# A decoder block with product-key experts: dots of gathered rows over three blocks instead of two, a gate turn in two halves, a tile of its own for third parts, and last sums written behind the last low parts

## The chip, the cores and the metric

The kernel runs on one core of a Trainium2 chip. Its time is the device time of one execution in microseconds; several executions are summed up by their median. The engines are named as in the profile: PE (TensorE, with PEld for its weight loads), DVE (VectorE), ACT (ScalarE), POOL (GpSimd) and SP (SyncE, which here only issues transfers). Each of the engines runs its own list of instructions in order, and waits at an instruction until what it reads has been written and what it overwrites has been read.

## What is computed

One layer on 512 tokens of width 1024, in float32. Two mixers (windowed attention and gated linear attention) come first, and what the change touches comes behind them: a layer of 16384 experts, of which each token uses 128.

```python
q = (h @ wq).reshape(B, S, 8, 2, 128)
sub_scores = einsum('bshpk,hpnk->bshpn', q, subkeys)
top_v, top_i = lax.top_k(sub_scores, 16)                 # 16 of 128 keys, for two halves of the key
cand   = top_v[..., 0, :, None] + top_v[..., 1, None, :] # 16 x 16 candidates of each head
best_v, best_pos = lax.top_k(cand, 16)
expert = take_along_axis(top_i[0] * 128 + top_i[1], best_pos)
gates  = softmax(best_v)
...
ub  = take(u, expert)                                    # 128 rows of u for each token
hid = gelu(einsum('tkd,td->tk', ub, h)) * gates
out = einsum('tk,tkd->td', hid, take(v, expert))
x   = rms_norm(x + gate2 * out)
```

The number of an expert is a pair of keys, each 0 to 127.

## The kernel before

**Two ways through the expert layer.** The tokens stand in four blocks of 128. For the first three ("dense" blocks 0, 1, 2; `DENSE`, 384 tokens) the kernel doesn't gather rows: it multiplies with all 16384 rows of `u` (in parts of 128 experts, "u parts"), and later with all rows of `v`, with a matrix of gates that is zero where a token doesn't use an expert. For the fourth block (`GB`) it gathers the rows of `u` and `v` that are used. In between stand the last 64 tokens of block 2 (`SB` is block 2, `TS` = 64): their part on the side of `u` is gathered too, in 64 steps, each a gather of 128 rows (`sp_gather`, an indirect transfer that POOL issues into one of three buffers, tile `spr`) and a product of these rows with the tokens with a sum along the row (`sp_dot`, one DVE instruction, L1292 in the profile of before). `sp_dot(m)` issues the gather for step m + 3, into the buffer that it has just read. When all 64 are done, `sp_finish` takes the gelu on ACT, `sp_close` multiplies with the gates of these tokens on DVE and writes the result over the gates with two transfers on SP's queue (`g<-sphid`). On the side of `v` these 64 tokens are dense like the others.

**Stages.** Modulation, mixers and the product-key scores take until about 425 us. From there to 797 us runs the **gate stage**, to 1460 us the **v stage**, and then the end. In the gate stage run, woven into each other:

- the gate matrix of the dense blocks, by groups of eight tokens, 48 groups in all. A group has a one-hot of keys on DVE (`one_hot`, L1182, tile `o12`, for both keys of each token), a product of the second key's one-hot with two parts of the gates on DVE (L1200, tile `o2`; the gates are split into three bf16 parts), eight third parts on ACT (L1204, one for each token, the one-hot with a scale per row), 24 matmuls on PE (L1211, banks `pg`), and two evictions on ACT (L1213, tile `gs`). Four groups (32 tokens) make a write of 2 MB to memory (`Gd<-gs`).
- what prepares the gates of a block: `gate_transposes` turns the two key numbers and the gates on PE so that tokens lie along the free axis (tile `t12`, bank `trg`), `gate_parts` and `gate_rest` split the gates into the parts (`gp3` the two that the product uses, `gr3` the third).
- the u parts: a high part on ACT (L71, `his`) and a low part on DVE (L72, `los`) of a chunk of rows of `u`, 24 matmuls on PE (L78 to L80, bank `ph`), a gelu on ACT (L967), and a write of the results (`gsp<-ge`) on ACT's queue.
- the 64 gathers and dots.

**Who sets the order.** In this stage DVE's and POOL's instructions run in the order in which the program writes them: `work` is a chain of generators that yield the DVE and PE time of each piece by a table of costs (a dot 1.15, a product 1.2, ...), and between two pieces a loop writes u parts as long as PE's share of its planned work is behind DVE's (`p * DVE_ALL < (d + LEAD_U) * PE_ALL`). PE, ACT and SP are ordered by a scheduler on a timeline of its own. `woven(n, rows, extra, rest)` writes a block: for q = 0 to 7 (16 tokens each) `gate_group` yields four pieces (one-hot, product and what follows, twice), and after each piece one dot is written while there are `rows`; behind q come the pieces of `extra[q]`. Before, dots are written 13 times ahead of block 0 (`head`) and then four times per q in blocks 0 and 1, until the 64 are used up in block 1 at q = 4. There `sp_finish` and `sp_close` follow (`second_block`, q = 4 and 5), then the turn of block 2's gates (q = 6 and 7), and block 2 has no dots.

**The v stage and the end.** `prep(i)` makes step i of the v stage ready: it multiplies gates with gelus (`A`), makes high parts on ACT (`hi` L1642, `Ah` L1645) and low parts on DVE (`lo` L1651, `Al` L1658), writes dots of the gathered block in between (`gather_to`), and loads what comes next. `v_matmuls` then runs, for each of the step's two key numbers, three matmuls into each of six accumulators (L78 to L80, `acc`). Tiles for the low parts: `slots`, three in turn (`los` twice, `lo2`). Three of the steps have `extras`, pieces that belong to the fourth block: `gate2_rows` (a table for the output gate), `table` with `close_half` (sum, gate and residual of the gathered block, L1688 to L1689, and its squares on ACT), and `root`, `refine`, `finish` (the norm: L1695 to L1706 on DVE, Ln and Exp on ACT (L1698), and the output, L1721). They are written between a step's high and low parts. The last four v numbers (`LAST`) are multiplied block by block, so that the first blocks are closed while the others run; then `close_half` and the norm for the three dense blocks.

## Time and profile before

| what | value |
|---|---|
| three runs, median (lowest to highest) | 1487.56 us (1485.44 to 1487.62) |
| the profiled execution, its own time | 1493.26 us |
| span of its instructions | 1491.5 us |
| mean granted TensorE clock | 0.978 |
| PE busy | 1430.0 us, 96% of the span, 9019 matmuls |
| DVE busy | 1259.9 us, 84% |
| ACT busy | 715.3 us, 48% |
| POOL busy | 608.1 us, 41% |
| DMA | 443.82 MB, mean 298 GB/s |

The shares are means over stages that differ: PE, for one, is nearly full in the v stage and less so in the gate stage. So the profile is read by stages. A row of a group of instructions has: line, engine, operation, result <- operands with their tile names (numbers left out), shapes, count | busy time, mean ns of one | idle time of the engine just ahead of them, and what ended most of it. A row of the timeline has: start in us, length, engine, line, operation, and in brackets the idle time ahead and what ended it. A row of windows has: the stretch, its length, busy us (and instructions) of PE, PEld, DVE, ACT and POOL, then the granted clock, the share of the DMA engines, and GB/s.

### The profile page before, as it was taken

The page shows a single profiled execution, that of the slowest core. Times are in us where ns is not written, and L with a number is a line of the kernel's source. Part 1 is how long each engine was busy: PE and PEld are TensorE (multiplying, and loading weights), DVE is VectorE, ACT ScalarE, POOL GpSimd, SP SyncE. Part 2 cuts the span into 40 slices and gives each one's busy share as a digit, 9 for nine tenths or more (in the row PEclk, how much of TensorE's full clock was granted, in tenths as well). Part 3 has the DMA queues.
Part 4 walks back from the last instruction along what each step waited for, and adds up shares of the span by engine and source line. Part 5 has one row for each costly group of instructions (what it writes and reads, how often), then busy time and mean ns, then how long its engine had stood idle before and what let it go on. Part 6 is the DMA issues. An engine that isn't in the chain of part 4 may idle for free. (4 is left out here: it accounts for less than half of the span.)

```text
span 1491.5 us, 23906 instructions
## 1 busy us (share of the span) xinstructions
PE 1430.0 (96%) x9019; PEld 1269.2 (85%) x9019; DVE 1259.9 (84%) x2306; ACT 715.3 (48%) x1297; POOL 608.1 (41%) x401
## 2 busy tenths in 40 slices
PE   5999999999999998989988999999999999999996
PEld 4788787888899998989988888888888888888885
DVE  6777767589999788989765899989899998899985
ACT  4556376533344577757996333332333333323232
POOL 2000000044523444532003677667777676555430
PEclk9999899999999999999999999999999999999998
DMA  9522636344258899999669999999999999999952
GB/s 356 227 85 81 203 101 210 120 178 160 102 192 275 309 348 323 362 351 308 231 227 390 415 411 412 412 413 410 401 410 388 407 371 412 401 412 410 384 224 71
DMA packets 129971, 443.82 MB, mean 298 GB/s; under 512 B 11952, under 2 KB 48576, under 8 KB 109504
## 3 DMA queue, kind: packets, MB, share of 16 engines
q1 hardware_dynamic: 71120, 256.39, 45.8%
q0 software_dynamic: 47136, 171.99, 29.8%
q10 hardware_dynamic: 11600, 13.93, 2.6%
q8 instruction: 70, 1.15, 0.3%
q14 instruction: 45, 0.37, 0.1%
HBM read 399.70 MB, written 42.47 MB: 296 GB/s over the span
## 5 line engine op out<-in xcount | busy, mean ns | idle before, releaser
L78 PE MATMUL ph<-h2Th,his 128*128 128x320 f32 x1024 | 323.0, 316 | 7.8 <-ACT ge L967 5.2
L80 PE MATMUL ph<-h2Th,los 128*128 128x320 f32 x1024 | 320.0, 314 | 10.3 <-DVE los L72 8.5
L79 PE MATMUL ph<-h2Tl,his 128*128 128x320 f32 x1024 | 319.6, 312 | 0.0
L1338 POOL DMA_INDIRECT gu<-in_u_dram,ix_u x128 | 210.5, 1645 | 174.7 <-DVE gu L1348 79.0
L1373 POOL DMA_INDIRECT gv<-in_vP_dram,ix_v x128 | 211.6, 1653 | 119.9 <-DVE gacc L1378 89.0
L80 PEld LDWEIGHTS ph<-h2Th,los 128*128 128x128 f32 x1024 | 195.6, 191 | 12.3 <-DVE los L72 10.2
L78 PEld LDWEIGHTS ph<-h2Th,his 128*128 128x128 f32 x1024 | 196.1, 192 | 9.9 <-ACT ge L967 6.0
L79 PEld LDWEIGHTS ph<-h2Tl,his 128*128 128x128 f32 x1024 | 196.0, 191 | 0.8
L1286 POOL DMA_INDIRECT spr<-in_u_dram,spix x64 | 106.1, 1658 | 167.6 <-DVE spr L1292 122.6
L79 PE MATMUL acc<-los,Ah 128*128 128x512 f32 x432 | 169.2, 392 | 2.4 <-DVE los L1651 2.4
L80 PE MATMUL acc<-his,Al 128*128 128x512 f32 x432 | 169.2, 392 | 0.1
L78 PE MATMUL acc<-his,Ah 128*128 128x512 f32 x432 | 168.8, 391 | 0.0
L1378 DVE SCALAR_TENSOR_TENSOR gacc<-gv,hg,gacc 128x1024 f32<-128x1024 f32 x127 | 162.4, 1278 | 3.2 <-DMA gv<-in_vP_dram,ix_v 2.6
L1348 DVE SCALAR_TENSOR_TENSOR gu<-gu,h2n 128x1024 f32<-128x1024 f32 x128 | 155.3, 1217 | 3.9 <-DMA gu<-in_u_dram,ix_u 3.9
L78 PE MATMUL acc<-hi,Ah 128*128 128x512 f32 x336 | 131.6, 392 | 0.0
L80 PE MATMUL acc<-hi,Al 128*128 128x512 f32 x336 | 131.3, 391 | 0.0
L79 PE MATMUL acc<-lo,Ah 128*128 128x512 f32 x336 | 130.9, 390 | 0.0
L1204 ACT ACTIVATE o<-o,gr 128x128 bf16<-128x128 bf16 x384 | 126.0, 447 | 4.8 <-DVE o L1182 4.8
L1645 ACT ACTIVATE Ah<-gr 128x768 fp32r<-128x768 f32 x64 | 53.5, 836 | 141.5 <-PE acc L79 127.3
L71 ACT ACTIVATE his<-u 128x1024 fp32r<-128x1024 f32 x86 | 90.7, 1058 | 32.5 <-DMA u<-in_uT_dram 15.6
L72 DVE TENSOR_TENSOR los<-u,his 128x1024 fp32r<-128x1024 f32 x75 | 91.2, 1218 | 15.8 <-ACT his L71 15.8
L1292 DVE SCALAR_TENSOR_TENSOR spr<-spr,xs 128x1024 f32<-128x1024 f32 x64 | 77.9, 1220 | 26.7 <-DMA spr<-in_u_dram,spix 26.6
(617 smaller groups left out, 3013.7 us busy)
## 6 DMA issues: line engine op xcount, KB each, us to landing
u<-in_uT_dram SPq DMA_DIRECT2D x43, 1024.0 KB, 6.4
gr<-Gd SPq DMA_DIRECT2D x15, 1536.0 KB, 10.9
Gd<-gs SPq DMA_DIRECT2D x10, 2048.0 KB, 10.7
gsp<-ge ACTq DMA_DIRECT2D x40, 320.0 KB, 5.2
wa<-in_w_ada_dram SPq DMA_DIRECT2D x12, 1024.0 KB, 5.3
wo<-in_w_out_dram SPq DMA_DIRECT2D x8, 1024.0 KB, 6.0
wq<-in_wq_dram SPq DMA_DIRECT2D x8, 1024.0 KB, 7.2
wi<-in_w_in_dram SPq DMA_DIRECT2D x7, 1024.0 KB, 5.0
```

What stands on the lines that cost most here:

```text
L71: nc.scalar.activation(hi, src, AF.Copy)
L72: lo_eng.tensor_tensor(lo, src, hi, OP.subtract)
L78: nc.tensor.matmul(acc, lh, rh, start=start, stop=False)
L79: nc.tensor.matmul(acc, lh, rl, start=False, stop=False)
L80: return nc.tensor.matmul(acc, ll, rh, start=False, stop=stop)
L1204: nc.scalar.activation(o2[:, g, 2, :, r], o12[:, g, 1, :, r], AF.Copy, scale=low[:, 2 * g0 + i:2 * g0 + i + 1])
L1286: nc.gpsimd.indirect_dma_start(out=sp[m], out_offset=None, in_=a["u"], in_offset=bass.IndirectOffsetOnAxis(ap=sp["ix", i][:, j:j + 1], axi ...
L1292: nc.vector.scalar_tensor_tensor(r, r, 1.0, sp["x", i], op0=OP.mult, op1=OP.mult, accum_out=sp["hid", i][:, j:j + 1])
L1338: nc.gpsimd.indirect_dma_start(out=ur, out_offset=None, in_=a["u"], in_offset=bass.IndirectOffsetOnAxis(ap=ix_u[:, s:s + 1], axis=0))
L1348: nc.vector.scalar_tensor_tensor(ur, ur, 1.0, h2n, op0=OP.mult, op1=OP.mult, accum_out=hid[:, s:s + 1])
L1373: nc.gpsimd.indirect_dma_start(out=vr, out_offset=None, in_=a["vP"], in_offset=bass.IndirectOffsetOnAxis(ap=ix_v[:, s:s + 1], axis=0))
L1378: nc.vector.scalar_tensor_tensor(gacc, vr, hg[:, s:s + 1], gacc, op0=OP.mult, op1=OP.add)
```

## The change

It has four edits.

1. **Dots.** A dot is written behind three of the four pieces of a q (`if i and rows`), and in block 2 too (`woven(SB, rows, ...)`). The head has 13 dots as before. The 64th is now written in block 2.
2. **The turn of block 2's gates.** `gate_transposes(n, t1)` turns the first t1 tokens' gates; `gate_turn(n, t0, t1)` is new and turns others. In block 1 (q = 6, 7) only the first 64 tokens of block 2 are turned and split; in block 2 follow `sp_finish` (q = 0), `sp_close` (1), the turn of the other 64 (2), their `gate_parts` (3), and `gate_rest` inside q = 4.
3. **Third parts** go to a tile `o3` of their own, [token][key], instead of the third slot of `o2`, where the keys of two tokens alternate. `o2` shrinks to its two parts.
4. **`prep`** writes its `extras` behind the low parts `lo` and `Al` instead of ahead of them.

The planner's cost of a product falls from 1.2 to 1.14 with it.

```diff
-    def gate_transposes(n):
+    def gate_transposes(n, t1=P):
...
-        pt = bank(f"trg{n}", BK[2])
-        nc.tensor.transpose(pt[:, :P], gates[n], ident)
...
-        nc.scalar.activation(gp3[:, :, 0], pair(pt[:, :P]), AF.Copy)
-        trs[n] = t12, gp3, pt, r
+        trs[n] = [t12, gp3, r, None]
         gate_transposes.tr = gate_transposes.tr or tr
-        yield 0, 0.6
...
+        yield from gate_turn(n, 0, t1)
+
+    def gate_turn(n, t0, t1):
+        pt = bank(f"trg{n}{t0}", BK[2])
+        nc.tensor.transpose(pt[:, t0:t1], gates[n][t0:t1], ident[t0:t1, t0:t1])
+        nc.scalar.activation(trs[n][1][:, t0 // 2:t1 // 2, 0], pair(pt[:, t0:t1]), AF.Copy)
+        trs[n][3] = pt
+        yield 0, 0.5
+
+    def gate_parts(n, t0=0, t1=P):
+        gp3, r, pt = (pair(t[:, t0:t1]) if len(t.shape) == 2 else t[:, t0 // 2:t1 // 2] for t in trs[n][1:])
+        nc.vector.tensor_tensor(r, pt, gp3[:, :, 0], OP.subtract)
+        nc.scalar.activation(gp3[:, :, 1], r, AF.Copy)
...
-            o2 = rt.tile([P, H, 3, P, 2], BF, tag="o2", bufs=3, name=f"o2_{n}{q}{t0}")
-            nc.vector.tensor_tensor(o2[:, :, :2], o12[:, :, 1, None].to_broadcast([P, H, 2, P, 2]),
+            o2 = rt.tile([P, H, 2, P, 2], BF, tag="o2", bufs=3, name=f"o2_{n}{q}{t0}")
+            o3 = rt.tile([P, TB, P], BF, tag="o3", bufs=3, name=f"o3_{n}{q}{t0}")
+            nc.vector.tensor_tensor(o2, o12[:, :, 1, None].to_broadcast([P, H, 2, P, 2]),
...
-                nc.scalar.activation(o2[:, g, 2, :, r], o12[:, g, 1, :, r], AF.Copy,
+                nc.scalar.activation(o3[:, i], o12[:, g, 1, :, r], AF.Copy,
                                      scale=low[:, 2 * g0 + i:2 * g0 + i + 1])
...
-                        nc.tensor.matmul(pt[:, i, :], o12[:, g, 0, :, r], o2[:, g, m, :, r],
+                        nc.tensor.matmul(pt[:, i, :], o12[:, g, 0, :, r], o2[:, g, m, :, r] if m < 2 else o3[:, 4 * f + i],
...
-    def woven(n, rows, extra, rest=()):
+    def woven(n, rows, extra, rests={}):
         for q in range(P // TG):
             for i, piece in enumerate(gate_group(DENSE.index(n), n, q)):
                 yield piece
-                yield from rest
-                if rows:
+                if i == 0 and q in rests:
+                    yield from rests[q]
+                if i and rows:
                     yield from sp_dot(rows.pop(0))
...
-    second_block = {1: [route(GB)], 2: [gathered_index()], 4: [sp_finish(0)], 5: [sp_close(0)],
-                    6: [gate_transposes(SB)], 7: [gate_parts(SB)]}
+    second_block = {1: [route(GB)], 2: [gathered_index()], 6: [gate_transposes(SB, P // 2)], 7: [gate_parts(SB, 0, P // 2)]}
     second_block[7].append(first_place())
-    third_block = {1: [first_gates()]}
+    third_block = {0: [sp_finish(0)], 1: [sp_close(0), first_gates()], 2: [gate_turn(SB, P // 2, P)],
+                   3: [gate_parts(SB, P // 2, P)]}
...
-                 woven(SB, [], third_block, gate_rest(SB)))
+                 woven(SB, rows, third_block, {0: gate_rest(SB, 0, P // 2), P // 2 // TG: gate_rest(SB, P // 2, P)}))
...
-        for piece in extra:
-            piece()
         nc.vector.tensor_tensor(lo, raw_, hi, OP.subtract)
         gather_to(due[i])
         activate()
...
             nc.vector.tensor_tensor(grp(Al), A, grp(Ah), OP.subtract)
             ready[i] = [(c + j, Ah[:, j], Al[:, j], hi[:, j], lo[:, j]) for j in range(2)]
+        for piece in extra:
+            piece()
         loads(i)
```

How it moves DVE's instructions is shown at three places. Each row below has the line, the operation, what it writes and reads, and the shape; `spr` with `sphid` is a dot, `los` a low part of a u part, `o12` a one-hot and `o2` a product. First, DVE in block 0, near its third q. Before:

```order
L1182 TENSOR_TENSOR o12_020_5456<-iot_3212,t120_4767 128x2048
L72 TENSOR_TENSOR los_2207<-u88_5458,his_2206 128x1024
L1292 SCALAR_TENSOR_TENSOR spr_4610,sphid0_4605<-spr_4610,xs0_4616 128x1024
L1200 TENSOR_TENSOR o2_020_5491<-o12_016_5381,gp30_4776 128x4x512
L1292 SCALAR_TENSOR_TENSOR spr_4610,sphid0_4605<-spr_4610,xs0_4616 128x1024
L72 TENSOR_TENSOR los_2207<-u88_5458,his_2206 128x1024
L1182 TENSOR_TENSOR o12_024_5560<-iot_3212,t120_4767 128x2048
L1292 SCALAR_TENSOR_TENSOR spr_4610,sphid0_4605<-spr_4610,xs0_4616 128x1024
L72 TENSOR_TENSOR los_2207<-u89_5564,his_2206 128x1024
L1200 TENSOR_TENSOR o2_028_5595<-o12_020_5456,gp30_4776 128x4x512
L1292 SCALAR_TENSOR_TENSOR spr_4610,sphid0_4605<-spr_4610,xs0_4616 128x1024
```

With the change:

```order
L1185 TENSOR_TENSOR o12_020_5458<-iot_3212,t120_4767 128x2048
L72 TENSOR_TENSOR los_2207<-u88_5460,his_2206 128x1024
L1204 TENSOR_TENSOR o2_020_5491<-o12_016_5382,gp30_4774 128x2048
L1296 SCALAR_TENSOR_TENSOR spr_4610,sphid0_4605<-spr_4610,xs0_4645 128x1024
L1185 TENSOR_TENSOR o12_024_5532<-iot_3212,t120_4767 128x2048
L1296 SCALAR_TENSOR_TENSOR spr_4610,sphid0_4605<-spr_4610,xs0_4645 128x1024
L72 TENSOR_TENSOR los_2207<-u88_5460,his_2206 128x1024
L1204 TENSOR_TENSOR o2_028_5565<-o12_020_5458,gp30_4774 128x2048
L1296 SCALAR_TENSOR_TENSOR spr_4610,sphid0_4605<-spr_4610,xs0_4645 128x1024
```

Of four dots the first, between the one-hot `o12_020` and the product `o2_020`, has gone; behind each later piece one dot stays.

Second, DVE where block 2 begins (`gr32` is the split of block 2's gates, `o12_20` its first one-hot, `trg2` or `trg20` the bank with the turned gates). Before:

```order
L1166 TENSOR_TENSOR gr32_7758<-trg2_7755,gp32_7757 128x128
L1182 TENSOR_TENSOR o12_20_7843<-iot_3212,t122_7748 128x2048
L1182 TENSOR_TENSOR o12_24_7845<-iot_3212,t122_7748 128x2048
L72 TENSOR_TENSOR los_2207<-u124_7679,his_2206 128x1024
L1174 TENSOR_TENSOR gr32_7758<-gr32_7758,gp32_7757 128x128
L1200 TENSOR_TENSOR o2_200_7877<-o12_20_7843,gp32_7757 128x4x512
L1182 TENSOR_TENSOR o12_28_7915<-iot_3212,t122_7748 128x2048
L1200 TENSOR_TENSOR o2_208_7917<-o12_24_7845,gp32_7757 128x4x512
```

With the change:

```order
L1296 SCALAR_TENSOR_TENSOR spr_4610,sphid0_4605<-spr_4610,xs0_4645 128x1024
L1170 TENSOR_TENSOR gr32_7682<-trg20_7683,gp32_7681 128x64
L1185 TENSOR_TENSOR o12_20_7837<-iot_3212,t122_7674 128x2048
L1185 TENSOR_TENSOR o12_24_7839<-iot_3212,t122_7674 128x2048
L72 TENSOR_TENSOR los_2207<-u124_7841,his_2206 128x1024
L1177 TENSOR_TENSOR gr32_7682<-gr32_7682,gp32_7681 128x64
L1204 TENSOR_TENSOR o2_200_7873<-o12_20_7837,gp32_7681 128x2048
L1296 SCALAR_TENSOR_TENSOR spr_4610,sphid0_4605<-spr_4610,xs0_4645 128x1024
L1185 TENSOR_TENSOR o12_28_7913<-iot_3212,t122_7674 128x2048
L72 TENSOR_TENSOR los_2207<-u124_7841,his_2206 128x1024
L1296 SCALAR_TENSOR_TENSOR spr_4610,sphid0_4605<-spr_4610,xs0_4645 128x1024
L1204 TENSOR_TENSOR o2_208_7945<-o12_24_7839,gp32_7681 128x2048
```

The split is 64 wide, dots stand ahead of it and behind it, and the last of them comes right behind the last row shown.

Third, DVE at the last steps of the v stage (`y3` are sums of the gathered block, `sm3` its norm, `los` and `lo2` low parts of `v`, `Al` low parts of gates). Before:

```order
L1688 TENSOR_TENSOR y3_13672<-gacc_8798,h2n_2199 128x512
L1689 TENSOR_TENSOR y3_13672<-y3_13672,xf3_13673 128x512
L1651 TENSOR_TENSOR lo2_8805<-v124__13451,hi2_8804 128x2048
L1658 TENSOR_TENSOR Al124_13669<-gr15_13279,Ah124_13668 128x24x2x16
L1636 TENSOR_TENSOR gr15_13279<-gp126_13449,gr15_13279 128x20x32
L1695 TENSOR_TENSOR sm3_13675<-sm3_13675 128x1
...
L1706 TENSOR_TENSOR sm3_13675<-sm3_13675 128x1
L1721 SCALAR_TENSOR_TENSOR y3_13672<-y3_13672,sm3_13675,fwb_13561 128x512 x2
L1651 TENSOR_TENSOR los_2207<-v126__13507,his_2206 128x2048
L1658 TENSOR_TENSOR Al126_13727<-gr15_13279,Ah126_13726 128x24x2x16
```

With the change:

```order
L1654 TENSOR_TENSOR lo2_8859<-v124__13505,hi2_8858 128x2048
L1661 TENSOR_TENSOR Al124_13723<-gr15_13333,Ah124_13722 128x24x2x16
L1693 TENSOR_TENSOR y3_13728<-gacc_8852,h2n_2199 128x512
L1694 TENSOR_TENSOR y3_13728<-y3_13728,xf3_13729 128x512
...
L1641 TENSOR_TENSOR gr15_13333<-gp126_13503,gr15_13333 128x20x32
L1654 TENSOR_TENSOR los_2207<-v126__13561,his_2206 128x2048
L1661 TENSOR_TENSOR Al126_13781<-gr15_13333,Ah126_13780 128x24x2x16
L1700 TENSOR_TENSOR sm3_13731<-sm3_13731 128x1
...
L1726 SCALAR_TENSOR_TENSOR y3_13728<-y3_13728,sm3_13731,fwb_13615 128x512 x2
```

The sums stand behind the low parts of pair 124, the norm and the output behind those of pair 126, the last one.

More of the change, by code (lines that the diff above doesn't have):

```diff
@@ L1144, in peer_block_kernel @@
     TB = 8
-    def gate_transposes(n):
+    pair = lambda v: v.rearrange("p (g r) -> p g r", r=2)
+    def gate_transposes(n, t1=P):
         t12 = rt.tile([P, P // 2, 2, 2], BF, tag="t12", bufs=2, name=f"t12{n}")
@@ L1151, in gate_transposes, with gate_rest @@
             tr = nc.tensor.transpose(pt[:, :P], I12[n][:, s], ident)
-            nc.scalar.activation(t12[:, :, s], pt[:, :P].rearrange("p (g r) -> p g r", r=2), AF.Copy)
-        pt = bank(f"trg{n}", BK[2])
-        nc.tensor.transpose(pt[:, :P], gates[n], ident)
+            nc.scalar.activation(t12[:, :, s], pair(pt[:, :P]), AF.Copy)
         gp3 = rt.tile([P, P // 2, 2, 2], BF, tag="gp3", bufs=2, name=f"gp3{n}")
         r = rt.tile([P, P], F32, tag="gr3", bufs=2, name=f"gr3{n}")
-        pair = lambda v: v.rearrange("p (g r) -> p g r", r=2)
-        nc.scalar.activation(gp3[:, :, 0], pair(pt[:, :P]), AF.Copy)
-        trs[n] = t12, gp3, pt, r
+        trs[n] = [t12, gp3, r, None]
         gate_transposes.tr = gate_transposes.tr or tr
-        yield 0, 0.6
-    def gate_parts(n):
-        gp3, pt, r = trs[n][1:]
-        pair = lambda v: v.rearrange("p (g r) -> p g r", r=2)
-        nc.vector.tensor_tensor(pair(r), pair(pt[:, :P]), gp3[:, :, 0], OP.subtract)
-        nc.scalar.activation(gp3[:, :, 1], pair(r), AF.Copy)
-        trs[n] = trs[n][0], gp3, None, r
+        yield from gate_turn(n, 0, t1)
[9 more added lines that the diff above has]
+        nc.scalar.activation(gp3[:, :, 1], r, AF.Copy)
+        trs[n][3] = None
         yield 0.25, 0
-    def gate_rest(n):
-        gp3, pt, r = trs[n][1:]
-        pair = lambda v: v.rearrange("p (g r) -> p g r", r=2)
-        nc.vector.tensor_tensor(pair(r), pair(r), gp3[:, :, 1], OP.subtract)
+    def gate_rest(n, t0=0, t1=P):
+        gp3, r = trs[n][1][:, t0 // 2:t1 // 2], pair(trs[n][2][:, t0:t1])
+        nc.vector.tensor_tensor(r, r, gp3[:, :, 1], OP.subtract)
         yield 0.25, 0
@@ L1188, in gate_group @@
     def gate_group(bi, n, q):
-        gp3, _, low = trs[n][1:]
+        gp3, low = trs[n][1:3]
         H = TB // 2
@@ L1215, in gate_group @@
             evicts.append(evict)
-            yield 1.2, 1.4
+            yield 1.14, 1.4
         k = bi * (P // TG) + q
@@ L1488, in peer_block_kernel @@
     rows = list(range(TS))
-    head = (route(SB), sp_index(0), sp_rows(0), between(route(0), (0, 0, 0)), gate_transposes(0), between(route(1), (2, 3, 3)),
+    head = (route(SB), sp_index(0), sp_rows(0), between(route(0), (0, 0, 0)), gate_transposes(0), between(route(1), (3, 3, 3)),
             between(gate_parts(0), (2,)), between(gate_rest(0), (2,)))
     first_block = {3: [gate_transposes(1)], 5: [gate_parts(1)], 6: [gate_rest(1)]}
-    second_block = {1: [route(GB)], 2: [gathered_index()], 4: [sp_finish(0)], 5: [sp_close(0)],
-                    6: [gate_transposes(SB)], 7: [gate_parts(SB)]}
+    second_block = {1: [route(GB)], 2: [gathered_index()], 6: [gate_transposes(SB, P // 2)], 7: [gate_parts(SB, 0, P // 2)]}
     second_block[7].append(first_place())
-    third_block = {1: [first_gates()]}
+    third_block = {0: [sp_finish(0)], 1: [sp_close(0), first_gates()], 2: [gate_turn(SB, P // 2, P)],
+                   3: [gate_parts(SB, P // 2, P)]}
     places = [(third_block, q) for q in range(P // TG - 1 - EARLY // 2, P // TG)]
@@ L1504, in peer_block_kernel @@
     work = chain(route_heads(), *head, woven(0, rows, first_block), woven(1, rows, second_block),
-                 woven(SB, [], third_block, gate_rest(SB)))
+                 woven(SB, rows, third_block, {0: gate_rest(SB, 0, P // 2), P // 2 // TG: gate_rest(SB, P // 2, P)}))
     NL_U = len(AHEAD) - LAST_U
-    DVE_ALL = 11 + 4 * 7.6 + 3 + 1.15 * TS + 2.34 * 2 * NGRP + 1.15 * EARLY + 1.14 * (NL_U - WQ_U)
+    DVE_ALL = 11 + 4 * 7.6 + 3 + 1.15 * TS + 2.28 * 2 * NGRP + 1.15 * EARLY + 1.14 * (NL_U - WQ_U)
     PE_ALL = 1.4 * 2 * NGRP + 3 + UCOST * (NL_U - WQ_U)
```

## The prediction

> **What bounds the kernel now.** I read the page, then the windows by stage (columns: stretch, length, then busy time and instructions of PE, PEld, DVE, ACT, POOL; PEclk, DMA share, GB/s).
>
> ```profile
> 440.00:520.00 80.00, 76.74 (x529) 76.55 (x529) 71.61 (x116) 37.73 (x73) 29.08 (x18) 0.98 0.82 284
> 520.00:702.00 182.00, 172.86 (x1489) 168.61 (x1488) 163.53 (x205) 131.56 (x316) 77.03 (x46) 0.98 0.94 338
> 702.00:797.00 95.00, 86.08 (x853) 81.17 (x852) 65.99 (x75) 89.17 (x255) 7.99 (x8) 0.93 0.74 253
> 797.00:1460.00 663.00, 660.14 (x3261) 571.71 (x3262) 596.23 (x620) 231.29 (x216) 416.50 (x251) 0.99 0.98 391
> 1460.00:1491.50 31.50, 19.11 (x69) 14.51 (x67) 19.53 (x41) 7.85 (x23) 0.00 (x0) 0.79 0.24 83
> ```
>
> From 797 to 1460 PE is busy 660 of 663 us: that stage can start earlier, but hardly shrink. What can shrink lies on both sides. In the gate stage (440 to 797) PE is idle 3.3 + 9.1 + 8.9 = 21.3 us, and the granted clock costs about 0.02 x 262 + 0.07 x 95 = 11.9 us more: **33 us below full pace**. Who holds it back differs between the halves. Two groups of DVE from 442 us to the last dot (702.6), then ACT's from there to 797 (count, busy time, mean ns of one, idle before them):
>
> ```profile
> L1292 DVE SCALAR_TENSOR_TENSOR spr<-spr,xs 128x1024 f32<-128x1024 f32 x64 | 77.9, 1220 | 26.7 <-DMA spr<-in_u_dram,spix 26.6
> L72 DVE TENSOR_TENSOR los<-u,his 128x1024 fp32r<-128x1024 f32 x57 | 69.5, 1219 | 0.0
> ```
> ```profile
> L1204 ACT ACTIVATE o<-o,gr 128x128 bf16<-128x128 bf16 x172 | 58.8, 464 | 0.0
> L1213 ACT ACTIVATE gs<-pg 128x512 f32<-128x512 f32 x46 | 27.5, 617 | 1.6 <-PE pg L1211 1.6
> L71 ACT ACTIVATE his<-u 128x1024 fp32r<-128x1024 f32 x9 | 9.6, 1091 | 0.0
> L967 ACT ACTIVATE ge<-ph 128x320 f32<-128x320 f32 x12 | 5.4, 446 | 1.9 <-PE ph L80 1.9
> ```
>
> Until the last dot **DVE leads**: it never waits for PE or ACT, only 26.6 us for gathered rows. After it **ACT leads**: busy 89.2 of 95 us, mostly with third parts (L1204), while DVE has room and PE starves. The dots keep DVE too full in the first half; the second has none.
>
> **The change, part by part.** *Dots spread.* What an instruction takes of its engine is the step to the next start:
>
> ```profile
> 703.68 1.22 DVE L1200 TENSOR_TENSOR o<-o,gp 128x2048 bf16<-128x2048 bf16 x1
> 704.81 1.22 DVE L1182 TENSOR_TENSOR o<-iot,t 128x2048 bf16<-128x2048 bf16 x1
> ```
> ```profile
> 700.12 1.08 ACT L1213 ACTIVATE gs<-pg 128x512 f32<-128x512 f32 x2
> 701.07 2.49 ACT L1204 ACTIVATE o<-o,gr 128x128 bf16<-128x128 bf16 x8
> L1204 ACT ACTIVATE o<-o,gr x384: 420/437/530, 507.3 to 789.6; 128x128 bf16<-128x128 bf16 x192
> ```
>
> A large DVE instruction takes 1.135 us. Two evictions take 0.95, and overlap by 0.13; a third part takes (2.49 - 0.44) / 7 = 0.293. A high part's mean 1.07 and a gelu's 0.45, less that overlap, are 0.95 and 0.32.
>
> By the order, DVE's last dot stands behind 57 low parts, 27 one-hots and 26 products now, behind 60, 35 and 34 with the change: 19 more, 21.6 us, and 0.3 for two narrow pieces: **+21.9**. Behind it remain 14 products for 22 and 8 low parts for 11. ACT's rest shrinks in step: 64 third parts, 16 evictions, 3 high parts and 3 gelus fewer, 18.8 + 7.6 + 2.9 + 1.0 = **-30.3**.
>
> *Waits for rows.* A gather may start when the dot three before it is done, so a landing has one turn of three dots. In 520 to 702 (the lines under the first tell idle time and landings):
>
> ```profile
> L1292 DVE SCALAR_TENSOR_TENSOR spr<-spr,xs x49: 1210/1219/1227, 519.7 to 701.4; 128x1024 f32<-128x1024 f32 x49
> ...
>   DMA spr<-in_u_dram,spix: 18.2, 12
> ...
> DMA to landing us min/median/max: 5.0/8.1/12.2
> ```
>
> DVE's work per dot is 163.5 / 49 = 3.34 us, a turn 10.0; the 21.9 us spread over 51 dots lengthen it to 11.3. Twelve waits hold 18.2 us, 1.5 each; each can lose 1.3. Upper bound 18.2 gone, lower bound none: three more gate writes of 2 MB leave before the last dot, 6.3 MB on top of 338 GB/s x 182 us = 61.5, at a DMA share of 0.94 already. I take **-11**, nearer to the upper end: of the longer turn 11.3 - 1.5 (dot and issue) = 9.8 are left for a landing, 1.7 more than the median 8.1, where today's 8.5 barely cover it. The 8.4 us of waits before 520 (26.6 - 18.2) stay: the same 13 dots precede the first product.
>
> *Gates turned late.* Today the third block's turn hangs on the last dots, and costs this, in ACT's half:
>
> ```profile
> 726.42 2.36 DVE L1182 TENSOR_TENSOR o<-iot,t 128x2048 bf16<-128x2048 bf16 x2 [5.00 <-ACT t L1152]
> ```
>
> The first 64 tokens no longer need the dots. The one-hot's wait now falls ahead of the last dot, on DVE's own path: between 0 and 5.0, I take the middle, **+2.5**. The turn of the other 64 adds a matmul, two ACT and two DVE instructions: 0.4 us of ACT, **+0.4**; DVE's two lie in its idle 29 us of the second half. Its two loads of gates stand on SP behind the load of the first gates; the price if they are late is a rival below.
>
> *Own places for third parts.* Same count; the write becomes contiguous. Nothing in the trace prices that: the nearest rows are a 128x128 activation without a per-row scale and a 512-wide one with it.
>
> ```profile
> L1167 ACT ACTIVATE gp<-gr x3: 310/310/344, 495.0 to 726.8; 128x128 bf16<-128x128 f32 x3
> ...
> L1712 ACT ACTIVATE w<-w,sm x3: 707/721/722, 1483.7 to 1487.1; 128x512 f32<-128x512 f32 x3
> ...
> 288.55 0.60 ACT L951 ACTIVATE h2n<-h2n 128x512 f32<-128x512 f32 x1 [0.75 <-PE h2n L950]
> ```
>
> The scale adds 721 - 597 = 124 ns to the wide one; 310 + 124 = 434 is what a third part lasts (437). So the stride explains nothing and I take **0**; were the whole 127 ns the stride's, 108 x 0.127 = 13.7 us of ACT would go, the other bound. No row shows a contiguous third part, so both ends stand in the range.
>
> *Last sums behind the last low parts.* Now:
>
> ```profile
> 1454.33 1.90 ACT L1642 ACTIVATE his<-v__13507 128x2048 fp32r<-128x2048 f32 x1
> ```
> ```profile
> 1451.81 0.96 DVE L1658 TENSOR_TENSOR Al<-gr,Ah 128x768 fp32r<-128x768 f32 x1 [1.61 <-ACT Ah L1645]
> ...
> 1460.30 0.22 DVE L1704 SCALAR_TENSOR_TENSOR sm<-sm 128x1 f32<-128x1 f32 x1 [5.49 <-ACT sm L1698]
> ...
> 1462.26 2.29 DVE L1651 TENSOR_TENSOR los<-v__13507,his 128x2048 fp32r<-128x2048 f32 x1
> 1464.47 0.95 DVE L1658 TENSOR_TENSOR Al<-gr,Ah 128x768 fp32r<-128x768 f32 x1
> 1468.86 0.69 DVE L1688 TENSOR_TENSOR y<-acc,h2n 128x512 f32<-128x512 f32 x1 [3.44 <-PE acc L80]
> ...
> 1473.49 0.69 DVE L1688 TENSOR_TENSOR y<-acc,h2n 128x512 f32<-128x512 f32 x1 [0.75 <-PE acc L80]
> ...
> 1481.65 0.69 DVE L1688 TENSOR_TENSOR y<-acc,h2n 128x512 f32<-128x512 f32 x1 [0.47 <-PE acc L80]
> ```
> ```profile
> 1461.79 0.39 PE L78 MATMUL acc<-his,Ah 128*128 128x512 f32 x1
> 1464.61 0.79 PE L79 MATMUL acc<-los,Ah 128*128 128x512 f32 x1 [2.43 <-DVE los L1651]
> ...
> 1471.45 0.39 PE L79 MATMUL acc<-lo,Ah 128*128 128x512 f32 x1
> 1471.68 0.39 PE L80 MATMUL acc<-hi,Al 128*128 128x512 f32 x1
> ```
>
> DVE sits 5.49 us behind ACT's root for the gathered block, with the low part of the last v pair queued behind it; PE waits 2.43 us, then runs sixteen steps in 1471.45 - 1461.79 = 9.66 us that take 16 x 0.23 = 3.7 at full pace: 6.0 us lost. With the change the pair's low part needs only its high part. ACT makes that after the gathered block's squares, whose sums now stand behind the previous Al: Al ends near 1452.7, four sums 1455.3, squares 1456.0, high part 1458, low part 1460.3, Al 1461.2: 1.7 us before PE wants the low part (1462.0), 1.1 before it wants Al. The moved root and output (0.3 + 0.6 + 0.5 + 1.4 us on DVE and ACT) end near 1464.3, where PE at full pace has the first accumulators. From there DVE needs the 1481.65 - 1468.86 = 12.8 us of now less the 1.2 it waited for PE: end near 1475.9 for 1481.65 (its last block's sums), so DVE keeps some half microsecond of PE's 6.0. **-5.5**; bounds 0 (low part late after all) and -6.0.
>
> [...]
>
> **Sum.** Gate stage +21.9 - 11 - 30.3 + 0.4 + 2.5 = -16.5; end -5.5; together -22.0. As a check, 16.5 is half of the 33 us below full pace: PE's own work does not stop it. The profiled execution took 1493.26 us (span 1491.5 and 1.8 around it), 5.7 above the median of the runs, 1487.56. So 1471.3 in its terms, **1465.6 us** in the median's.
>
> **Rivals.** *The gathers bind instead* (slower). If landings lengthen with the queue, every turn waits for rows. It decides from a mean landing of those 9.8 us; at the longest seen, 12.2, each of 17 turns loses 2.4, 41 us for the 18.2 now: gate stage +21.9 + 22.8 - 30.3 + 2.9 = +17.3, with the end +11.8, 1499. It breaks even at a landing near 11.5. For it: DMA share 0.94 and 6.3 MB more. Against: the v stage moves 391 GB/s, and the median landing is 8.1. Chance 0.08.
>
> *The waits stay as they are*: what the turn gains, the queue takes. Gate stage -16.5 + 11 = -5.5, total -11.0: 1476.6. For it: ACT's u loads also came late in that half, and keep doing so. Chance 0.20.
>
> *The second half of the turn comes late.* On SP its two loads stand behind the load of the first gates, and that behind a gate write:
>
> ```profile
> SPq L1234 <- DMA Gd<-gs: 10.0, 1, 10.0
> ```
> ```profile
> g<-sphid SPq DMA_DIRECT2D x2, 16.0 KB, 4.8
> ```
>
> PE stands in order before that transpose. Between that write and the transpose PE has five gate groups and four u parts to do; 23 groups (46 evictions) and 12 parts (gelus) took it 86 us after the last dot, so these take 19 to 28, for 10 + 4.8 = 15 of transfers (wait and median landing); if the margin goes, a stall of some 6 us and 3 of half clock: -13, 1474.6. Chance 0.08.
>
> *The stride was the third parts' cost*: up to 13.7 more, of which PE's remaining 16 us give perhaps half: 1458.5. Chance 0.06.
>
> **Chances.** Forecast 0.58, with its own range 1459 to 1472 (waits 4 to 18 gone, one-hot 0 to 5). The range for 8 in 10 takes the third-part rival and most of the two weaker gains: 1457 to 1481. A difference under 0.2% (3 us) can't be told from none here. Slower by that: the gathers, 0.08, and a little for an order that misfits, 0.09. Same: a weak end of the second rival, 0.05. Faster: 0.86.
>
> **What would show it.** Right: DVE's wait for spr rows under 19 us in all (26.6 now); the last dot 7 to 16 us later than 702.5, the first L1647 high part of the v stage some 16 earlier than 796; third parts still 0.43 us; PE's idle in the gate stage near half of 21; no wait at the last los, and PE's last matmul some 22 earlier than 1481. Wrong: spr waits of 25 us or more, landings over 9 us; PE waiting at the 64-wide transpose; ACT's third parts near 0.31.

## The result

The changed kernel takes 1467.9 us (median of 4 runs, 1465.6 to 1469.7) beside 1486.5 for the kernel before (4 runs, 1484.4 to 1487.6): 18.6 us less, a ratio of 0.9876 with a 95% interval of 0.9855 to 0.9896. Forecast were 22.0 us less, 1465.6.

The two profiled executions differ by more, 1491.5 and 1465.0 us of span. Part of that lies ahead of everything that the change touches. These are the windows up to the first matmul of a u part, of before and of after (length, busy time and instructions of PE, PEld, DVE, ACT, POOL, then the granted clock):

```profile
0.00:304.20 304.20, 280.49 (x2042) 234.51 (x2043) 216.37 (x492) 164.56 (x345) 15.77 (x34) 0.97 0.49 173
```
```profile
0.00:297.60 297.60, 271.60 (x2043) 226.55 (x2044) 217.57 (x492) 164.69 (x345) 15.45 (x34) 1.00 0.50 177
```

The instructions are the same, and the 6.6 us go with a granted clock of 0.97 in one execution and 1.00 in the other (20.5 us at half clock in the first, none in the second). So stages are compared below, not spans. The stages of after:

```profile
440.00:520.00 80.00, 75.13 (x513) 74.66 (x511) 69.16 (x113) 36.91 (x72) 29.78 (x19) 0.96 0.80 280
520.00:714.50 194.50, 189.38 (x1739) 184.81 (x1738) 181.42 (x223) 158.94 (x397) 75.15 (x45) 1.00 0.96 348
714.50:776.60 62.10, 56.34 (x575) 52.15 (x573) 43.48 (x56) 59.19 (x171) 9.90 (x7) 1.00 0.77 263
776.60:1440.00 663.40, 659.77 (x3264) 571.18 (x3263) 598.80 (x620) 232.66 (x215) 411.19 (x251) 1.00 0.98 391
```

The last dot ends at 714.5 (702.6 before; counted from the first u-part matmul, it is 18.5 later), and the v stage starts at 776.6 (796.1). ACT's stretch in between has shrunk from 93.5 to 62.1 us. ACT still leads in it, 59.2 of 62.1 us, by these groups:

```profile
L1208 ACT ACTIVATE o<-o,gr 128x128 bf16<-128x128 bf16 x113 | 38.2, 463 | 0.0
L1217 ACT ACTIVATE gs<-pg 128x512 f32<-128x512 f32 x32 | 19.9, 650 | 0.5 <-PE pg L1215 0.5
```

113 third parts stand where 172 stood, and 32 evictions for 46. Up to the last dot DVE still waits for rows, and for nothing else. Its groups from the 13th dot to the last (the 13th, with its own wait of 4.8 us, counted in):

```profile
L1296 DVE SCALAR_TENSOR_TENSOR spr<-spr,xs 128x1024 f32<-128x1024 f32 x52 | 63.4, 1219 | 17.7 <-DMA spr<-in_u_dram,spix 17.7
L72 DVE TENSOR_TENSOR los<-u,his 128x1024 fp32r<-128x1024 f32 x44 | 53.6, 1218 | 0.0
L1185 DVE TENSOR_TENSOR o<-iot,t 128x2048 bf16<-128x2048 bf16 x35 | 42.4, 1219 | 0.0
```

In the whole stage these waits are 23.7 us in 16 places, where they were 26.6 in 18. At the end of the v stage the low part of the last pair (`los`) now comes early. DVE, then PE:

```profile
1437.59 2.29 DVE L1654 TENSOR_TENSOR los<-v__13561,his 128x2048 fp32r<-128x2048 f32 x1 [1.86 <-ACT his L1647]
1439.80 0.95 DVE L1661 TENSOR_TENSOR Al<-gr,Ah 128x768 fp32r<-128x768 f32 x1
...
1442.15 1.42 DVE L1726 SCALAR_TENSOR_TENSOR y<-y,sm,fwb 128x512 f32<-128x512 f32 x2
1443.60 0.69 DVE L1693 TENSOR_TENSOR y<-acc,h2n 128x512 f32<-128x512 f32 x1
...
1455.16 0.69 DVE L1693 TENSOR_TENSOR y<-acc,h2n 128x512 f32<-128x512 f32 x1
```
```profile
1441.36 0.39 PE L78 MATMUL acc<-his,Ah 128*128 128x512 f32 x1
1441.58 0.39 PE L79 MATMUL acc<-los,Ah 128*128 128x512 f32 x1
```

PE takes the low part 0.22 us after the step before it, at full clock (0.39 us a matmul), where it waited 2.43 us and then ran at half clock (0.79 and 0.63 us a matmul, a granted clock of 0.50 from 1465 to 1470 us). DVE's closing sums (1443.60) follow right behind the output of the gathered block, without a wait.

### The profile page after: what moved, and what is told of

Read it like the earlier page. It is cut to its first block, busy times and chain, and to the rows that moved or that the text cites. A ratio compares the mean times of both kernels' runs of the same rounds, so it can differ in the third digit from the quotient of the medians.

```text
span 1465.0 us, 23919 instructions
## 1 busy us (share of the span) xinstructions
PE 1408.5 (96%) x9020; PEld 1250.4 (85%) x9020; DVE 1261.0 (86%) x2308; ACT 716.0 (49%) x1299; POOL 603.1 (41%) x401
## 5 line engine op out<-in xcount | busy, mean ns | idle before, releaser
L1377 POOL DMA_INDIRECT gv<-in_vP_dram,ix_v x128 | 206.5, 1613 | 115.5 <-DVE gacc L1382 90.1
L1208 ACT ACTIVATE o<-o,gr 128x128 bf16<-128x128 bf16 x384 | 121.6, 416 | 7.8 <-DVE o L1185 7.8
L1296 DVE SCALAR_TENSOR_TENSOR spr<-spr,xs 128x1024 f32<-128x1024 f32 x64 | 77.9, 1219 | 23.7 <-DMA spr<-in_u_dram,spix 23.7
```

The lines of the kernel that those rows point to most:

```text
L1208: nc.scalar.activation(o3[:, i], o12[:, g, 1, :, r], AF.Copy, scale=low[:, 2 * g0 + i:2 * g0 + i + 1])
L1296: nc.vector.scalar_tensor_tensor(r, r, 1.0, sp["x", i], op0=OP.mult, op1=OP.mult, accum_out=sp["hid", i][:, j:j + 1])
L1377: nc.gpsimd.indirect_dma_start(out=vr, out_offset=None, in_=a["vP"], in_offset=bass.IndirectOffsetOnAxis(ap=ix_v[:, s:s + 1], axis=0))
```

## The experiments

Twelve more kernels were run. The table has their medians, their ratio to the kernel before on the same chip, and the stages of each profiled execution, read from its timeline: "head" from the first u-part matmul to the 13th dot, "body" to the last dot, "tail" to the first high part of the v stage, "v" to the last matmul, and DVE's waits for rows in all. The sum of head, body and tail is the gate stage. Names: each is explained below.

| kernel | median | ratio (95%) | head | body | tail | gate | v | waits |
|---|---|---|---|---|---|---|---|---|
| before | 1486.5 | 1 | 207.5 | 190.9 | 93.5 | 491.9 | 685.5 | 26.6 |
| third parts alone | 1485.4 | 1.0003 (0.9985 to 1.0020) | 207.5 | 189.4 | 92.3 | 489.2 | 683.6 | 25.3 |
| end alone | 1478.7 | 0.9965 (0.9944 to 0.9985) | 207.9 | 189.0 | 91.7 | 488.6 | 678.6 | 25.1 |
| after | 1467.9 | 0.9876 (0.9855 to 0.9896) | 207.4 | 209.5 | 62.1 | 479.0 | 678.5 | 23.7 |
| end back | 1472.0 | 0.9913 (0.9888 to 0.9938) | 206.2 | 211.4 | 59.0 | 476.6 | 684.1 | 24.7 |
| four | 1479.8 | 0.9970 (0.9946 to 0.9993) | 206.2 | 196.5 | 88.8 | 491.5 | 678.6 | 30.6 |
| rows before | 1462.3 | 0.9844 (0.9801 to 0.9887) | 200.2 | 174.8 | 96.9 | 471.9 | 682.0 | 1.3 |
| rows after | 1458.1 | 0.9810 (0.9768 to 0.9853) | 196.6 | 205.8 | 62.9 | 465.3 | 679.2 | 0.0 |
| thirds on DVE | 1467.0 | 0.9868 (0.9834 to 0.9902) | 205.5 | 211.8 | 58.0 | 475.3 | 678.6 | 21.1 |
| head 10 | 1467.2 | 0.9888 (0.9853 to 0.9924) | 210.4 | 198.0 | 68.9 | 477.3 | 679.5 | 21.9 |
| thin | 1468.1 | 0.9885 (0.9860 to 0.9911) | 206.3 | 209.9 | 61.4 | 477.6 | 679.2 | 23.1 |
| four buffers | 1458.2 | 0.9811 (0.9788 to 0.9834) | 200.9 | 202.2 | 65.1 | 468.2 | 679.3 | 5.6 |
| four buffers, thirds | 1458.2 | 0.9801 (0.9775 to 0.9827) | 199.6 | 211.3 | 57.7 | 468.6 | 678.6 | 4.7 |
| four buffers before | 1474.1 | 0.9929 (0.9904 to 0.9954) | 203.4 | 177.6 | 95.3 | 476.3 | 684.2 | 9.5 |

The change also has an edit that the diff ahead of the prediction leaves out: `between(route(1), (2, 3, 3))` became `(3, 3, 3)`. So the head has 13 dots with the change and had 12 before, where the 13th stood behind the first two one-hots of block 0. A kernel with the old dots and one with the new ones therefore compare by their last dot (head and body together) and by their gate sum, not by head or body alone; for "head 10", with its own order, only the gate sum compares with others. Three kernels have the gate stage of before (one with the other tile for third parts, which shows no price) and ran it in 491.9, 489.2 and 488.6, mean 489.9; three have that of after but for what does not touch it (after, end back, thin): 479.0, 476.6, 477.6, mean 477.7. So one profile tells a stage to some 2 us, and the gate stage lost **12.2 us**. The v stage had a mean of 684.4 with the late sums (before, third parts alone, end back) and 678.8 without (after, thin, end alone): **5.6 us**. Together 17.8, beside 18.6 in the medians.

### Which edit it was

*End back*: after, with the pieces ahead of the low parts again.

```diff
         if i > 1:
             gather_to((before + due[i] + 1) // 2)
+        for piece in extra:
+            piece()
         nc.vector.tensor_tensor(lo, raw_, hi, OP.subtract)
...
-        for piece in extra:
-            piece()
         loads(i)
```

> The changed kernel with one edit undone: the pieces of the gathered block stand ahead of the low parts again. My theory: the last low part of v is late again, PE waits some 2.4 us for it and runs some 15 matmuls at half clock behind it, so 5.5 to 7 us slower than the changed kernel, about 1474 (median of the changed kernel 1467.9). Rival A, only the wait counts: 2.4 slower, 1470. Rival B, the end was hidden by DVE's closing sums: no difference.

1472.0: slower than after by 4.1 us in the medians, by 5.5 in the ratios and by 5.6 in the v stage of the two profiles, so at or under the low end of what I expected. The wait is back to the hundredth. PE's timeline:

```profile
1444.08 0.79 PE L79 MATMUL acc<-los,Ah 128*128 128x512 f32 x1 [2.43 <-DVE los L1656]
...
1446.82 0.63 PE L78 MATMUL acc<-his,Ah 128*128 128x512 f32 x1
1447.25 0.52 PE L79 MATMUL acc<-los,Ah 128*128 128x512 f32 x1
1447.61 0.40 PE L80 MATMUL acc<-his,Al 128*128 128x512 f32 x1
```

This time half clock lasted about 3.4 us behind the wait, not the 6.8 of the profile before, so it cost 1.7 in place of 3.4. That makes 2.43 + 1.7 = 4.1 for the edit in this execution; most of the rest of the 5.6 is half clock at the start of the v stage (6.8 us of it here, 3.4 in after), which this edit doesn't touch. Rival B (hidden) falls. Rival A, the wait alone at 2.4, leaves out the half clock that stands in the rows above; the times alone would hardly tell 2.4 from 4.1. How much half clock follows differs between executions: of the five profiles with the late low part, each with this wait of 2.43 us, one has 6.8 us of it behind the wait (before), three have 3.4 (end back, third parts alone, four buffers before), and "rows before" has none.

*End alone*: before, with the same edit and nothing else.

> The kernel before with that edit alone. My theory: the edits don't touch each other, so 5.5 to 7 us faster than before, about 1480.5 for 1486.5, and no wait of PE at the last low part. Rival A: 2.4 faster. Rival C, the end only pays because the gate stage ended earlier and dots of the gathered block were through sooner: no gain here.

0.9965, so 5.2 us faster (2.2 to 8.3; 7.7 by the medians), and no wait at the last low part. The edit pays by itself, and rival C falls. The interval takes in rival A's 2.4.

*Third parts alone*: before, with the tile `o3`.

```diff
-            o2 = rt.tile([P, H, 3, P, 2], BF, tag="o2", bufs=3, name=f"o2_{n}{q}{t0}")
+            o2 = rt.tile([P, H, 2, P, 2], BF, tag="o2", bufs=3, name=f"o2_{n}{q}{t0}")
+            o3 = rt.tile([P, TB, P], BF, tag="o3", bufs=3, name=f"o3_{n}{q}{t0}")
...
-                nc.scalar.activation(o2[:, g, 2, :, r], o12[:, g, 1, :, r], AF.Copy,
+                nc.scalar.activation(o3[:, i], o12[:, g, 1, :, r], AF.Copy,
```

> The kernel before with the third parts in a tile of their own, and nothing else. With the change a third part lasts 0.40 us in place of 0.44, yet eight of them still start 0.293 apart. My theory: only the spacing fills ACT, so no difference (within 3 us). Rival: the 38 ns of 384 third parts, 14.6 us, were part of the gain; of them the 170 or so in the ACT-bound part count, some 6.5 us faster.

1.0003, no difference, and its interval (0.9985 to 1.0020) excludes a gain of over 2.2 us. The row of its third parts, and after's, with eight of them in a row from after's timeline:

```profile
L1205 ACT ACTIVATE o<-o,gr x384: 384/397/512, 502.1 to 781.0; 128x128 bf16<-128x128 bf16 x192
```
```profile
L1208 ACT ACTIVATE o<-o,gr x384: 384/399/530, 506.2 to 770.3; 128x128 bf16<-128x128 bf16 x192
```
```profile
684.87 2.45 ACT L1208 ACTIVATE o<-o,gr 128x128 bf16<-128x128 bf16 x8
```

One is 38 ns shorter (437 before), but eight take 2.45 us: (2.45 - 0.40) / 7 = 0.293 from start to start, as before. What filled ACT was the step, and the step did not change.

*Four*: after, with four dots to a q, so that the last dot comes in block 1 again, and the late turn kept.

```diff
-                if i and rows:
+                if rows:
...
-between(route(1), (3, 3, 3))
+between(route(1), (2, 3, 3))
```

> The changed kernel with four dots to each 16 tokens again, so that the last dot comes in block 1; the late second turn, the third parts and the end stay as changed. My theory: the rate of the dots made the gate stage's gain, so 10 to 13 us of it are gone, about 1479; DVE's last dot some 12 us earlier, waits for rows back near 26 us in all. Rival: the gain came from turning half of the gates ahead of the dots' results, which took DVE's waits of 3.3 and 5.0 us at the start of the third block away: then at most 5 us are lost, 1473 or less.

1479.8, near "end alone" (1478.7): the gate stage is back at 491.5. So the rival (at most 5 us lost) falls: the gate stage's gain hung on the rate of the dots, and the late turn, still there, gave none that shows. A part of what "four" loses is the late turn's own price, though: at 741.46 us PE waits 1.92 us for the loads of the second half (`g<-sphid`), and 3.4 us of half clock follow, up to 3.6 us in all. DVE's waits even grew:

```profile
L1296 DVE SCALAR_TENSOR_TENSOR spr<-spr,xs 128x1024 f32<-128x1024 f32 x64 | 78.0, 1221 | 30.7 <-DMA spr<-in_u_dram,spix 30.6
```

### What the waits for rows are worth

*Rows after* and *rows before*: all dots read the first gathered buffer and write the two others, and 61 of 64 gathers are not issued; the hidden values of the 64 tokens are left out.

```diff
-        r = sp.pop(m)
-        nc.vector.scalar_tensor_tensor(r, r, 1.0, sp["x", i], op0=OP.mult, op1=OP.mult,
+        r, w = sp["r"][:, 0], sp["r"][:, 1 + m % 2]
+        nc.vector.scalar_tensor_tensor(w, r, 1.0, sp["x", i], op0=OP.mult, op1=OP.mult,
...
-        if m + 3 < TS:
-            sp_gather(m + 3)
-        elif m == TS - 1:
+        if m == TS - 1:
```

> The changed kernel without 61 of the 64 gathers: every dot reads the first gathered buffer and writes another one, so DVE's work is the same and only rows and their 32 MB of transfers are missing (the hidden values of those 64 tokens are left out). It prices what the waits for rows still cost (23.7 us of DVE's time, 12.6 of them behind the 13th dot). My theory: DVE leads up to the last dot, so most of the 23.7 come off, up to the 19 us that PE loses in the gate stage to idle time and half clock: 10 to 17 us faster than the changed kernel, 1451 to 1458. Rival: the waits are cover, PE and ACT would be no earlier: under 4 us.

> The same with the kernel before (61 of 64 gathers left out, dots on one buffer). It waited 26.7 us for rows. My theory: DVE leads there until the last dot and ACT behind it, with nothing between them to give time back, so 20 to 27 us faster than before, 1460 to 1466; then part of what the change gains could have been had from the rows alone. Rival: only the DVE time of the dots matters, under 8 us.

Rows after: 1458.1, 9.8 us faster than after, just under what I expected. Rows before: 0.9844, 23.2 us faster, as expected. Their windows, from 520 to the last dot and from there to the v stage, first with the change:

```profile
520.00:703.90 183.90, 183.90 (x1697) 180.37 (x1695) 173.90 (x215) 152.34 (x382) 0.00 (x0) 1.00 0.66 227
703.90:766.70 62.80, 58.20 (x581) 53.14 (x578) 43.43 (x54) 59.93 (x174) 9.84 (x7) 1.00 0.79 273
```
```profile
520.00:671.50 151.50, 151.50 (x1333) 149.36 (x1332) 148.21 (x189) 116.22 (x281) 0.00 (x0) 1.00 0.64 221
671.50:768.50 97.00, 86.85 (x896) 81.11 (x894) 65.68 (x75) 91.70 (x262) 9.31 (x7) 0.98 0.73 246
```

Without waits PE never idles from 520 us to the last dot, with or without the change. What is left of the spreading then is the tail: PE loses 97.0 - 86.9 = 10.1 us there without it and 62.8 - 58.2 = 4.6 with it. Gate stage against gate stage the spreading gains 471.9 - 465.3 = 6.6 us when there is nothing to wait for, and 12.2 with real rows. So by these profiles about half of its gain is the balance of the two halves, and the rest is there only with the waits. The times don't settle that split: without rows the whole change, its end included, is worth 4.2 us in the medians (1462.3 to 1458.1), where gate and v stage of the two profiles give 6.6 + 2.8 = 9.4, and the four runs of each kernel differ in their mean granted clock (0.994 and 0.991).

These runs also drop 32 MB of traffic. *Four buffers* keeps it and gives a row more time instead. Its space comes from `o2`, so *thin* is its control.

```diff
-            o2 = rt.tile([P, H, 2, P, 2], BF, tag="o2", bufs=3, name=f"o2_{n}{q}{t0}")
+            o2 = rt.tile([P, H, 2, P, 2], BF, tag="o2", bufs=2, name=f"o2_{n}{q}{t0}")
...
-            for j in range(3):
+            for j in range(4):
...
-        sp[m] = sp["r"][:, m % 3]
+            sp["r2"] = rt.tile([P, 1, D], F32, name="sprx")
+        sp[m] = sp["r"][:, m % 4] if m % 4 < 3 else sp["r2"][:, m % 4 - 3]
...
-        if m + 3 < TS:
-            sp_gather(m + 3)
+        if m + 4 < TS:
+            sp_gather(m + 4)
```

> The changed kernel with four gather buffers in place of three, so that a row has a turn of four dots to land; the space comes from tile o2, two buffers in place of three. Without any gathers the changed kernel ran at 1458.1, 9.8 us faster, which is the most that this can give. My theory: the turn grows from some 11 to 15 us, and the waits for rows (23.7 us) fall below 8: 4 to 9 us faster than the changed kernel, 1459 to 1464. Rival: landings lengthen with what is under way, as the queue is full (DMA share 0.97 in that stretch): waits stay above 18, within 2 us.

> The control of the last: the changed kernel with two buffers for o2 in place of three, and three gather buffers as they are. A product then waits for PE to be through with the product two groups back; PE stands one to two groups behind DVE in the trace. My theory: 0 to 3 us slower than the changed kernel, 1468 to 1471. Rival: products wait often, 5 us or more slower, and four gather buffers would then gain more than their own run shows.

Thin (the `o2` line alone): 1468.1, no price. Four buffers: **1458.2**, 9.9 us faster than thin, and all that leaving out the gathers gave. The dots of its two tiles, and how long rows took to land with four buffers and, last, with three (thin):

```profile
L1297 DVE SCALAR_TENSOR_TENSOR spr<-spr,xs 128x1024 f32<-128x1024 f32 x48 | 58.3, 1217 | 5.2 <-DMA spr<-in_u_dram,spix 5.2
L1297 DVE SCALAR_TENSOR_TENSOR sprx<-sprx,xs 128x1024 f32<-128x1024 f32 x16 | 19.5, 1216 | 0.4 <-DMA sprx<-in_u_dram,spix 0.4
```
```profile
DMA to landing us min/median/max: 5.6/8.9/13.9
```
```profile
DMA to landing us min/median/max: 4.9/7.8/12.0
```

Landings did lengthen with one more row under way, by 1.1 us, but the turn lengthened by a whole dot's share, and the waits fell from 23.1 to 5.6. The rival (a full queue gives nothing) falls.

*Four buffers before*: the same on the kernel before, without the change.

> The kernel before with four gather buffers in place of three (and two for o2), and nothing of the change. Without gathers it ran at 1462.3, 23.5 us faster. My theory: the change and a fourth buffer take the same waits; at four dots to 16 tokens a turn grows from 10 to some 13 us, over landings of 8 to 9, so that 16 to 22 us are gained here, 1464 to 1470, as much as the whole change brings. Rival: with dots that dense the turn stays too short or landings lengthen with it, and half of the waits stay: 8 to 13 us, 1473 to 1478.

0.9929, 10.5 us faster (6.8 to 14.3): my expectation was missed, and the rival's number came, though not its reason. The waits did go, by some 16 us (9.5 for a mean of 25.7):

```profile
L1293 DVE SCALAR_TENSOR_TENSOR spr<-spr,xs 128x1024 f32<-128x1024 f32 x48 | 58.6, 1221 | 5.5 <-DMA spr<-in_u_dram,spix 5.4
L1293 DVE SCALAR_TENSOR_TENSOR sprx<-sprx,xs 128x1024 f32<-128x1024 f32 x16 | 19.5, 1222 | 4.1 <-DMA sprx<-in_u_dram,spix 4.1
```

Head and body are 4.2 and 12.2 us shorter than the means of the three kernels with this gate stage, but the tail is 2.8 longer (95.3 for 92.5): more third parts are left for ACT behind the last dot (176, for 168 to 172), though 2.8 us are little more than one profile tells. With four buffers on both sides the spreading is worth 476.3 - 468.2 = 8.1 us of gate stage. A fourth buffer doesn't replace it; by the times the two add (10.5 us here, 18.6 for the change, 28 for both), by the gate stages of the profiles they overlap by some 4 (13.6 and 12.2, 21.7 for both).

### What is left

*Thirds on DVE*: after, with the third parts of every second group of block 2 as one DVE product.

```diff
+            on_dve = n == SB and t0 > 0
+            o3v = o3.rearrange("p t k -> p (t k)").rearrange("p (g k r) -> p g k r", g=H, r=2)
+            if on_dve:
+                nc.vector.tensor_tensor(o3v, o12[:, :, 1], gate_rest.g3[:, g0:g0 + H, None].to_broadcast([P, H, P, 2]),
+                                        OP.mult)
-            for i in range(TB):
+            for i in range(TB) if not on_dve else ():
```

> The changed kernel, with the third parts of every second group of block 2 (8 of 16 groups, 64 third parts) made by one DVE product each from a bf16 copy of the third gate part. It takes 64 x 0.293 = 18.7 us from ACT, in the stretch behind the last dot where ACT is busy 78 of 95 us, and adds 8 x 0.6 = 4.8 us to DVE, which is idle 12 us there. My theory: ACT leads there, so PE's idle time of some 6 us behind the last dot mostly goes: 3 to 6 us faster than the changed kernel, 1462 to 1465. Rival: PE itself has no more to give there, or DVE takes ACT's place: within 2 us.

1467.0, not told apart from after. The tail, from the last dot:

```profile
715.00:773.10 58.10, 56.77 (x599) 55.16 (x596) 48.63 (x65) 42.19 (x107) 11.18 (x9) 1.00 0.82 282
```

ACT falls to 42.2 of 58.1 us and PE's idle time to 1.3, so ACT did lead there; but in the profiles that was worth 2.8 us of tail (58.0 for a mean of 60.8) against a body 1.5 longer (211.8 for 210.3), and nothing that the times show. *Four buffers, thirds* (both):

> Four gather buffers and two for o2, and the third parts of eight groups of block 2 made on DVE. My theory: with the waits for rows gone, ACT's stretch behind the last dot is a larger part of what is left, so the two add: 6 to 12 us faster than the changed kernel, 1456 to 1462. Rival: PE is the bound by then (without gathers it was idle only 4.6 us in the gate stage), so the third parts add nothing to the four buffers.

1458.2, the same as four buffers alone: the gate stage is 468.6 and 468.2. The rival's number came. Its reason, that PE has no more to give, is not what the profiles show: behind the last dot PE's idle time fell from 7.2 to 1.3 us, but ahead of it, from the 13th dot on, it is 6.1 us for 1.4. So idle time moved from one half to the other.

*Head 10*: after, with ten dots ahead of block 0 and one more at q = 2, 4 and 6 of blocks 0 and 1.

```diff
-between(route(1), (3, 3, 3))
+between(route(1), (2, 2, 2))
...
-                if i and rows:
+                if (i or n < SB and q in (2, 4, 6)) and rows:
```

> The changed kernel with 10 dots ahead of block 0 in place of 13, and one dot more at each of six places in blocks 0 and 1 (q = 2, 4, 6). Ahead of the first product DVE waits 10.8 us for rows, and PE then waits 4.9 us at 509 us. My theory: three turns fewer there bring block 0 forward, 2 to 5 us faster, 1463 to 1466. Rival: the waits come back at the places with four dots: no difference within 2 us, or slower.

1467.2, no difference; the gate stage is 477.3 for 477.7. The waits moved rather than went (21.9 us). The second half of the turn was late here as in "four" (1.92 us), by little:

```profile
727.62 0.24 PE L1163 MATMUL trg<-ident,g 64*128 64x64 f32 x1 [1.52 <-DMA g<-sphid]
```

## Why the prediction was right, step by step

The time (1467.9 for 1465.6), the sign and the place were right. The means over like kernels, as above, give each term its size:

| term | forecast | shown |
|---|---|---|
| DVE's longer way to the last dot, without waits | +21.9 | +21.3 (the last dot 19.5 later, and 1.8 less of waits) |
| waits for rows | -11 (0 to -18.2) | -1.8 (25.7 to 23.8): -3.4 behind the 13th dot, +1.5 up to it |
| one-hot of block 2 on DVE's way | +2.5 | 0 |
| ACT's tail, with its 0.4 | -29.9 | -31.7 (92.5 to 60.8) |
| third parts' own places | 0 | 0 |
| end | -5.5 | -5.6 in the profiles; -5.5 (end back) and -5.2 (end alone) by the ratios, -4.1 and -7.7 by the medians |
| sum | -22.0 | -17.8 by the profiles, -18.6 in the medians |

The waits missed by 9 us. The one-hot and the tail came out 4.3 us better than forecast, and the forecast started from a median of before that was 1.1 us above the later one. So that the time came within 2.3 us is in part luck.

- **Who leads where** held: DVE to the last dot (busy 181.4 of 194.5 us from 520 us on, and waiting for nothing but rows), ACT behind it (59.2 of 62.1). "Four" shows that the rate of the dots carries the gate stage's gain, and the runs without rows show that DVE's waits do reach the end.
- **The step that failed is the term for waits.** It took the mean turn (10.0 to 11.3 us) against the median landing, and so expected most landings to fit. Behind the 13th dot the waits fell by only 3.4 us (18.3, 16.8 and 16.4 in the three profiles; then 12.9, 15.1 and 13.3), so the second rival ("the waits stay as they are", 1476.6) was nearer on this term than the forecast. The turn itself grew as forecast, by 1.3 us: read dot by dot from the traces, its mean behind the 13th dot is 9.7 us in before and 11.0 in after and in thin. Had each of the twelve waits of before lost those 1.3 us, some 5 of 18.2 would be left. So what failed is the assumption that landings would stay as they were: from the free buffer to the landed row, a gather behind the 13th dot took a mean of 8.1 us in before and 8.7 in thin (the trace of after has no landings), and the longest quarter over 9.5 and over 10.4. That is one trace each, and what lengthened the landings was not tested; the DMA share rose from 0.94 to 0.96 in that stretch. The 1.5 us more up to the 13th dot go with that dot's move: with two one-hots fewer ahead of it, DVE waited for it a mean of 4.3 us where it waited 1.8. The fourth buffer, which adds a whole dot's share to every turn, took most of the waits.
- **The one-hot** of block 2 never waited for the turn ahead of the last dot; what one-hots wait now (4.05 us once, for PE) falls in the tail, where DVE has time.
- **The end** held in place and, within the spread of the runs, in size: the queue of the low part behind ACT's root was the cause, and PE's half clock a part of its price (3.4 us lost to it in before, 1.7 in "end back"). The forecast took that part from one profile with 6.8 us of half clock, the longest of the five.
- **The stride** had no price, since the step from start to start, 0.293 us with either way of writing, is what counts; the sign "third parts still 0.43 us" was nevertheless wrong, as one lasts 0.40.
- **Gathers that bind**: the waits for rows did not grow with the change. **The second half late**: not in the changed kernel, but by 1.5 us in "head 10" and by 1.9 in "four". The 3 us of half clock that the rival sets behind a stall of 6 us no run shows; in "four" 3.4 us at half clock, 1.7 us lost, stood behind the 1.9.
- Of the signs, waits under 19 us (23.7) and PE's idle time near half (in the gate stage's windows 21.3 before, 15.8 after) did not come: the loss to half clock fell more than the idle time did, from 11.9 to 3.2 us by the same windows, but that is mostly the difference between two executions: "third parts alone" and "end alone", with the gate stage of before, spent 6.8 us of it at half clock, as after did, where before spent 23.9. Those two stood some 28 us below full pace (25 of idle time, 3.4 of clock), not the 33 on which the forecast checked its sum.

## What to carry to other kernels

When one engine leads in the first half of a stage and another in the second, move the work that can move until both halves lose the same; count that by instructions and steps from start to start, which came out within 2 us here. The waits on a ring of three buffers weren't cured by a tenth more time for each turn, which took 1.8 of 25.7 us here: give such a ring one more buffer (here 9.9 us for 4 KB a partition, taken from a ring that didn't need its third), and do both, as each still paid on top of the other. Pieces that hang on another engine's answer belong behind what the main engine needs next, not ahead of it.
